# A two-layer hybrid decoder trunk on one core: no two-input GpSimd work, one gate moved inside a merge, and two matmul stages with the features outermost

## The chip, the cores and the metric

One core of a Trainium2 chip runs the whole program. Times are device microseconds (us) of one execution. PE is TensorE (PEld its weight loads), DVE VectorE, ACT ScalarE, POOL GpSimd, SP SyncE, which issues nearly all DMAs. Lower is better.

## The reference, cut to what matters

The input x is 256 tokens of 1024 features in float32. Each of two layers does:

```python
h = rmsnorm(x, mix_norm)
ret, fox, rwkv, gate = split(h @ w_in)               # 1024, 772, 1024, 3072 columns
y = retention(ret), forgetting_attention(fox), rwkv7(rwkv)   # 256 columns each
merged = sum(sigmoid(gate[b]) * (y[b] @ p[b]) for b in range(3))
x = x + merged @ w_out
h = rmsnorm(x, ffn_norm)
x = x + (silu(h @ w_gate) * (h @ w_up)) @ w_down      # 2816 columns in between
```

In the RWKV branch the columns are first mixed with those of the token before: `cols + (prev - cols) * mu`.

## The kernel before, in words

**Layout and precision.** Activations are kept with the features on the partitions: x is four tiles `x0_0` to `x0_3` of 128 x (2 x 256), two blocks of 128 features in each. A product is made from three fp32r matmuls on split operands (`mm3`, L286): a high part (`whi`, `xh`) rounded by an ACT copy, a low part (`wlo`, `xl`) left over by a DVE subtraction, and hi x hi + hi x lo + lo x hi into one accumulator. A block is one 128x128 piece of weights with its three matmuls of 256 columns; a pair (`gemm_pair`, L296) is two output blocks over all eight feature blocks, 16 blocks or 48 matmuls, into one accumulator tile. Another order is `gemm_halves` (L308): with `kcut` it runs the feature blocks below the cut for both outputs first, then the rest.

**Weights.** `weights` (L222) yields all weight tiles in the order of use. `_piece` (L256) starts the DMA of the next tile on SP's queue (three buffers `raw`, 1 MB for 16 blocks) and splits eight blocks: an ACT cast to `whi` (L273), a DVE subtraction to `wlo` (L274), in four buffers each. `refill` (L280) keeps three split pieces ahead of the matmuls.

**Order.** The kernel is written as a list of operations; a scheduler orders each engine's queue at build time, by priority (roughly the order of writing; `early` raises it) and by what it expects to be ready. Each queue then runs strictly in that order, with semaphores. The RWKV, FoX and retention branches are generators that `mixers` (L496) interleaves with the dense matmuls of `gemms` (L529) by written-out costs (`PACE`); `self.need` makes it finish a branch before the merge that uses it.

**The stages of a layer.** (a) The norm is folded in afterwards: `norm_start`, `norm_add` (L384) scale and split x, `norm_sum` adds squares, `rstd` (L409) sums over partitions with the `pn` matmuls and takes an inverse root on DVE, `replicate` (L426) spreads it with the `pss` matmul. (b) Four RWKV pairs (`mixers`, L500 to L507, and `rwkv_in`, L622): the first as `gemm_halves` with a cut at 7, each needing all of x; then `rwkv_in` scales by rstd and mixes with the previous token, where POOL makes `dd` (L644) and DVE the rest (L633). (c) FoX (`fox_in`, L963; `mqk`, `mv`), retention (`ret_in`) and twelve gate pairs, with the branches in between. In `rwkv` (L655) POOL makes `k2` (L730), copies of v (L735), `rs` (L740) and `nn` (L786); the bonus matmul `pb` (L748) waits for `rkk` (L745, DVE); `lora` is loaded at L668 and used by `pw` (L673). In `ret` (L1103) the four `rsw` DMAs shift `rqk`, `cs` is loaded, POOL multiplies by the cosine (L1116), DVE by the sine (L1117). (d) Gates in the order of the branches; behind the second branch's gates the merges of branches 0 and 1, behind the third's four gates the four merges of branch 2, 12 matmuls each (L564). A merge is `(gate + 1) * ps` on DVE (L567), an addition (L569) on POOL, for branch 2 from the second tile on on DVE, and for branch 2 a split into `hi` and `lo` (L572), whose `lo` of the first tile is on POOL. (e) w_out (`layer`, L482): four pairs over the merged tiles, the first with a cut at 4, the last as halves. (f) The FFN.

**The start.** A memset tile feeds 30 dummy matmuls (L169). SP issues `x0_0`, the parameters, half of the first weight tile, `x0_1`, the other half, `x0_2`, `x0_3` (L175 to L183), then the next tiles and the constants (`load_rest`).

Of the kernel before, what the change touches and what calls it, by code (L numbers as in the profile page):

```python
# [91 lines left out]
def pack_inputs(inp, depth=DEPTH):  # L92
# [40 lines left out]
    out["win"] = np.ascontiguousarray(np.stack(win))  # L133
# [17 lines left out]
class Kernel:  # L151
    def __init__(self, ctx, tc, d, depth=DEPTH, debug=None):
# [16 lines left out]
        for _ in range(30):  # L169
# [4 lines left out]
        self.xt = [self.xp.tile([P, 2, T], F32, tag="x", bufs=5, name=f"x0_{j}") for j in range(4)]  # L174
        nc.sync.dma_start(self.xt[0], d["xt"][:, 0:2, :])  # L175
        nc.sync.dma_start(par[0], d["par"][0, :, 0:P_RES])
        self.jobs, self.raws, self.ready, self.cur = list(self.weights()), [], [], []
        w0 = self.raw.tile([P, 2080], F32, tag="raw", name=self.nm("raw"))
        for j in range(4):
            if j:  # L180
                nc.sync.dma_start(self.xt[j], d["xt"][:, 2 * j:2 * j + 2, :])
            if j < 2:
                nc.sync.dma_start(w0[:, 1024 * j:1024 * (j + 1)], d["win"][0, 0, :, 1024 * j:1024 * (j + 1)])  # L183
        self.jobs[0:1] = [(w0, 4, P, 0), (w0, 4, P, 4), (w0, 8, P, 8)]
# [123 lines left out]
    def gemm_halves(self, xs, kcut=None, hook=None, tag="mm"):  # L308
# [14 lines left out]
        for lo, hi in ((0, kcut), (kcut, n)):  # L323
# [139 lines left out]
    def layer(self, l):  # L463
        tc, nc, d = self.tc, self.nc, self.d
        if l == 0:
            self.norm_start(0, "mixg")
            for j in range(4):
                self.norm_add(j, False)
                if j != 2:
                    self.piece()  # L470
        xs = self.xs
        with ExitStack() as st:
# [23 lines left out]
    def mixers(self, l, xs):  # L496
# [3 lines left out]
        ps = [self.gemm_halves(xs, 7, tag="rw")]  # L500
        if l == 0:
            self.load_rest()
        for _ in range(1):
            ps.append(self.run(self.gemm_pair(xs)))
        rn, dg = self.rstd()
        ps.append(self.run(self.gemm_pair(xs)))
        rstd = self.replicate(dg)  # L507
# [21 lines left out]
    def gemms(self, l, xs, rstd, rn):  # L529
# [11 lines left out]
        gates = {}  # L541
        for b in (0, 1, 2):
            for c in range(4):
                gen = self.gemm_pair(xs)
                while True:
                    try:
                        next(gen)
                    except StopIteration as e:
                        ps = e.value
                        break  # L550
                    yield PACE["gemms3"]
                g = gates[b, c] = self.big.tile([P, 2, T], F32, tag="gate", bufs=8, name=self.nm("gate"))
                nc.vector.tensor_tensor(out=g, in0=ps, in1=self.b2(rstd), op=ALU.mult)  # L553
                nc.scalar.activation(g, g, AF.Tanh, scale=0.5)
                yield PACE["gemms3"]
            if b == 0:
                continue
            for bb in ((0, 1) if b == 1 else (2,)):
                self.need = ("ret", "fox", "rwkv")[bb]
                yield PACE["gemms4"]  # L560
                self.need = None
                y = [(self.y[bb][0][:, k, :], self.y[bb][1][:, k, :]) for k in range(2)]
                for c in range(4):
                    ps = self.run(self.gemm_pair(y))  # L564
                    g, m = gates[bb, c], gates[0, c]
                    with self.early("hp_merge"):
                        nc.vector.scalar_tensor_tensor(out=g, in0=g, scalar=1.0, in1=ps, op0=ALU.add, op1=ALU.mult)  # L567
                        if bb:
                            (nc.vector if bb == 2 and c >= 1 else nc.gpsimd).tensor_tensor(out=m, in0=m, in1=g, op=ALU.add)  # L569
                    if bb == 2:  # L570
                        with self.early("hp_turn"):
                            hi, lo = self.split(self.t2, m, [P, 2, T], ("t2", "t2"), nc.gpsimd if c < 1 else nc.vector)  # L572
                        self.mx.extend((hi[:, i, :], lo[:, i, :]) for i in range(2))
                    elif c % 2:
                        yield PACE["gemms5"]

# [45 lines left out]
    def rwkv_in(self, l, xs, rstd, first):  # L622
        nc = self.nc
        rav = self.big.tile([P, 2 * NC, 3 * C], F32, tag="q6", bufs=1, name=self.nm("rav"))
        r = self.t512("r")
# [5 lines left out]
        def mix(j, pj, dd):  # L631
            for i in range(2):
# [564 lines left out]
```

## Time and profile before

| | us |
|---|---|
| median of three runs | 800.0 (799.88 to 800.56) |
| profiled execution, its own time | 800.76 |
| its span, first to last instruction | 799.0 |
| PE busy | 783.6 (98%) |
| DVE busy | 576.2 (72%) |
| ACT busy | 397.1 (50%) |
| POOL busy | 61.6 (8%) |

Matmul records overlap: each lasts longer than the distance to the next one's start, so a busy PE can still change its pace, and a hole between two records is shorter than the time that was lost. The other engines run one instruction after the other.

### The profile page before, as it was taken

The numbers are of one execution on the slowest core, as the hardware profiler recorded it, in microseconds if no ns is written. First come the engines' busy times: TensorE is split into PE (matmuls) and PEld (weight loads), VectorE is DVE, ScalarE is ACT, GpSimd is POOL, SyncE is SP. The second block draws the span as 40 slices with busy tenths as digits, with TensorE's granted clock in tenths as the row PEclk, the third lists the DMA queues.
The fourth block names the chain that finished last, engine by engine and source line by source line (L and its number), as shares of the span: only waits on it lengthen the run. The fifth ranks groups of instructions, "written<-read, shape, count | busy, mean of one in ns | idle before, by whom it ended". The sixth has DMA issues, their size and how long they took to land.

```text
span 799.0 us, 16543 instructions
## 1 busy us (share of the span) xinstructions
PE 783.6 (98%) x7018; PEld 762.5 (95%) x7018; DVE 576.2 (72%) x900; ACT 397.1 (50%) x543; POOL 61.6 (8%) x83
## 2 busy tenths in 40 slices
PE   8999899999999999999999999999999999999998
PEld 6999899999999999999998988999999999999997
DVE  5897979597867666656678798877878666666453
ACT  6367445535645444445444764554456545444331
POOL 3201210031000000000023030101110000000000
PEclk9999999999999999999999999999999999999999
DMA  8565524335454554556554553452445454555650
GB/s 308 208 226 167 170 80 169 140 114 205 161 208 167 203 205 172 191 184 211 200 188 175 197 172 106 162 174 106 142 176 190 180 201 174 206 202 164 211 190 27
DMA packets 27802, 140.42 MB, mean 176 GB/s; under 512 B 7600, under 2 KB 9168, under 8 KB 12496
## 3 DMA queue, kind: packets, MB, share of 16 engines
q1 hardware_dynamic: 27728, 139.36, 50.2%
q8 instruction: 55, 0.90, 0.5%
q14 instruction: 19, 0.16, 0.1%
HBM read 136.97 MB, written 1.33 MB: 173 GB/s over the span
## 4 chain that ended last, share of the span: by engine, by line
PE 88%; DVE 6%; DMA 2%; ACT 1%; issue 1%; POOL 1%; SPq 0%; POOLq 0%; DVEq 0%; ACTq 0%
PE mm L290 26%; PE mm L294 25%; PE mm L293 25%; DVE wlo L274 2%; PE mqk L439 1%; PE mqk L438 1%; PE mqk L437 1%; ACT whi L273 1%; DMA rsw<-rqk 1%; PE pgm L762 1%; DVE rkk L745 1%; DMA raw<-in_win 1%; DMA raw<-in_pp 1%; PE mv L437 1%; PE mv L439 1%
## 5 line engine op out<-in xcount | busy, mean ns | idle before, releaser
L273 ACT CAST whi<-raw 128x1024 fp32r<-128x1024 f32 (+1 forms) x257 | 264.7, 1033 | 321.7 <-PE mm L293 232.2
L274 DVE TENSOR_TENSOR wlo<-raw,whi 128x1024 fp32r<-128x1024 f32 (+1 forms) x257 | 313.3, 1221 | 143.0 <-ACT whi L273 142.3
L290 PE MATMUL mm<-xh,whi 128*128 128x256 f32 x1312 | 368.0, 280 | 0.5 <-ACT whi L273 0.5
L294 PE MATMUL mm<-xh,wlo 128*128 128x256 f32 x1248 | 346.3, 277 | 0.7 <-DVE wlo L274 0.7
L293 PE MATMUL mm<-xl,whi 128*128 128x256 f32 x1248 | 346.3, 278 | 0.0
L290 PEld LDWEIGHTS mm<-xh,whi 128*128 128x128 f32 x1312 | 246.6, 188 | 2.8 <-issue 0.9
L294 PEld LDWEIGHTS mm<-xh,wlo 128*128 128x128 f32 x1248 | 234.4, 188 | 1.1 <-DVE wlo L274 0.9
L293 PEld LDWEIGHTS mm<-xl,whi 128*128 128x128 f32 x1248 | 234.5, 188 | 0.8 <-issue 0.5
L290 PE MATMUL mm<-hi,whi 128*128 128x256 f32 x576 | 160.1, 279 | 0.0
L294 PE MATMUL mm<-hi,wlo 128*128 128x256 f32 x544 | 150.9, 277 | 0.0
L293 PE MATMUL mm<-lo,whi 128*128 128x256 f32 x544 | 150.8, 277 | 0.0
L290 PEld LDWEIGHTS mm<-hi,whi 128*128 128x128 f32 x576 | 108.2, 188 | 0.6 <-issue 0.3
L294 PEld LDWEIGHTS mm<-hi,wlo 128*128 128x128 f32 x544 | 102.1, 188 | 0.2
L293 PEld LDWEIGHTS mm<-lo,whi 128*128 128x128 f32 x544 | 102.1, 188 | 0.1
L569 POOL TENSOR_TENSOR gate<-gate,gate 128x512 f32<-128x512 f32 x10 | 13.3, 1336 | 142.3 <-DVE gate L567 142.3
L600 DVE TENSOR_TENSOR h<-t,mm 128x512 f32<-128x512 f32 x22 | 15.1, 687 | 11.5 <-PE mm L294 8.6
L567 DVE SCALAR_TENSOR_TENSOR gate<-gate,mm 128x512 f32<-128x512 f32 x24 | 16.1, 682 | 8.6 <-PE mm L294 8.5
L597 DVE TENSOR_TENSOR t<-mm,rstd 128x512 f32<-128x512 f32 (+1 forms) x24 | 15.2, 645 | 8.5 <-PE mm L294 8.5
L553 DVE TENSOR_TENSOR gate<-mm,rstd 128x512 f32<-128x512 f32 x24 | 16.5, 689 | 3.8 <-PE mm L294 3.5
L293 PE MATMUL mm<-xh,wlo 128*128 128x256 f32 x64 | 18.0, 281 | 0.7 <-DVE wlo L274 0.7
L439 PE MATMUL mv<-whi,xl 128*128 128x260 f32 (+1 forms) x64 | 18.6, 290 | 0.0
L437 PE MATMUL mv<-whi,xh 128*128 128x260 f32 (+1 forms) x64 | 18.6, 290 | 0.0
(259 smaller groups left out, 797.9 us busy)
## 6 DMA issues: line engine op xcount, KB each, us to landing
raw<-in_wg SPq DMA_DIRECT2D x44, 1024.0 KB, 4.7
raw<-in_wgate SPq DMA_DIRECT2D x24, 1024.0 KB, 4.8
raw<-in_wd SPq DMA_DIRECT2D x16, 1024.0 KB, 5.0
raw<-in_win SPq DMA_DIRECT2D x13, 1024.0 KB, 8.0
raw<-in_wo SPq DMA_DIRECT2D x8, 1024.0 KB, 4.8
raw<-in_pp SPq DMA_DIRECT2D x6, 1024.0 KB
raw<-in_wd SPq DMA_DIRECT2D x8, 768.0 KB, 4.3
raw<-in_wqk SPq DMA_DIRECT2D x4, 1024.0 KB, 5.0
```

Source lines behind the costliest of these rows:

```text
L273: nc.scalar.copy(hi[:, :m * width], r)
L274: nc.vector.tensor_tensor(out=lo[:, :m * width], in0=r, in1=hi[:, :m * width].bitcast(F32), op=ALU.subtract)
L290: nc.tensor.matmul(out, wh, xh, start=first, stop=False)
L293: nc.tensor.matmul(out, wh, xl, start=False, stop=False)
L294: nc.tensor.matmul(out, wl, xh, start=False, stop=last)
L437: nc.tensor.matmul(out, xh[:, s], wh, start=first, stop=False)
L439: nc.tensor.matmul(out, xl[:, s], wh, start=False, stop=last)
L553: nc.vector.tensor_tensor(out=g, in0=ps, in1=self.b2(rstd), op=ALU.mult)
L567: nc.vector.scalar_tensor_tensor(out=g, in0=g, scalar=1.0, in1=ps, op0=ALU.add, op1=ALU.mult)
L569: (nc.vector if bb == 2 and c >= 1 else nc.gpsimd).tensor_tensor(out=m, in0=m, in1=g, op=ALU.add)
L597: nc.vector.tensor_tensor(out=t[:, o, :], in0=p, in1=self.bs(rstd, o), op=ALU.mult)
L600: nc.vector.tensor_tensor(out=h, in0=t, in1=pu, op=ALU.mult)
```

## The change

1. The first three weight tiles of layer 0's four RWKV pairs (and the fourth) are repacked, and `first_pairs` runs the four pairs with the feature blocks outermost: two feature blocks for all eight outputs, then the next two. `norm_add` of x tile 1, 2, 3 and `load_rest` are written between them, `rstd` and `replicate` inside the last quarter. The first quarter of the first tile is issued from ACT's queue; 22 dummy matmuls instead of 30.
2. `gemm_quad` runs w_out's first two pairs in the same manner, in both layers.
3. The last gate (branch 2, tile 3) moves behind the first two merges of branch 2; the RWKV projection's weights are loaded in two halves.
4. POOL's two-input work goes to DVE, its copies of v to ACT, and the token mixing becomes an ACT scaling by 1 - mu and one DVE operation. POOL keeps memsets and small one-input work.
5. `lora` is loaded at the top of `rwkv_in`.

```diff
-        for _ in range(30):
+        for _ in range(22):
             nc.tensor.matmul(pz, zero[:, 0:P], zero, start=True, stop=True)
...
+        nc.scalar.dma_start(w[0][:, 0:512], d["win0"][0, :, 0:512])
         nc.sync.dma_start(self.xt[0], d["xt"][:, 0:2, :])
         nc.sync.dma_start(par[0], d["par"][0, :, 0:P_RES])
...
+        nc.sync.dma_start(w[0][:, 512:1024], d["win0"][0, :, 512:1024])
+        nc.sync.dma_start(w[0][:, 1024:2048], d["win0"][0, :, 1024:2048])
+        for j in range(1, 4):
+            nc.sync.dma_start(self.xt[j], d["xt"][:, 2 * j:2 * j + 2, :])
+            if j < 3:
+                nc.sync.dma_start(w[j][:, 0:2048], d["win0"][j])
+        self.jobs[0:3] = [(w[0], 4, P, 0), (w[0], 4, P, 4), (w[0], 8, P, 8), (w[1], 16, P, 0), (w[2], 16, P, 0)]
...
+    def first_pairs(self, xs):
+        ps = [self.ps.tile([P, 2, T], F32, tag=t, bufs=n, name=self.nm("mm")) for t, n in (("rw", 2), ("rw", 2), ("mm", 4), ("mm", 4))]
+        for kk in range(4):
+            if kk < 3:
+                self.norm_add(kk + 1, False)
+            if kk == 2:
+                self.load_rest()
+            for j in range(4):
+                if kk == 3 and j == 1:
+                    rn, dg = self.rstd()
+                if kk == 3 and j == 3:
+                    rstd = self.replicate(dg)
+                for m in range(2):
+                    for k in range(2 * kk, 2 * kk + 2):
+                        if not self.cur:
+                            self.refill()
+                        self.mm3(ps[j][:, m, :], self.block(), xs[k], k == m == 0, k == KT - 1 and m == 1)
+        return ps, rn, rstd
+
+    def gemm_quad(self, xs):
+        ps = [self.ps.tile([P, 2, T], F32, tag="mm", bufs=4, name=self.nm("mm")) for _ in range(2)]
+        for kk in range(KT // 2):
+            for j in range(2):
+                for m in range(2):
+                    for k in range(2 * kk, 2 * kk + 2):
...
+                        self.mm3(ps[j][:, m, :], self.block(), xs[k], k == m == 0, k == KT - 1 and m == 1)
...
                 if j == 0:
-                    ps = self.gemm_halves(mx, 4)
...
+                    both = self.gemm_quad(mx)
+                ps = both[j] if j < 2 else self.run(self.gemm_pair(mx)) if j == 2 else self.gemm_halves(mx)
...
+        def merge(bb, c):
...
+                nc.vector.scalar_tensor_tensor(out=g, in0=g, scalar=1.0, in1=ps, op0=ALU.add, op1=ALU.mult)
+                if bb:
+                    nc.vector.tensor_tensor(out=m, in0=m, in1=g, op=ALU.add)
+            if bb == 2:
+                with self.early("hp_turn"):
+                    hi, lo = self.split(self.t2, m, [P, 2, T], ("t2", "t2"))
...
         for b in (0, 1, 2):
             for c in range(4):
+                if b == 2 and c == 3:
+                    self.need = "rwkv"
+                    yield PACE["gemms4"]
+                    self.need = None
+                    for m in (0, 1):
+                        merge(2, m)
+                for _ in gate(b, c):
                     yield PACE["gemms3"]
...
+        for c in (2, 3):
+            merge(2, c)
...
+        lora = self.t512("lora")
+        nc.sync.dma_start(lora.rearrange("p a t -> p (a t)"), self.d["par"][l, :, P_RES:])
...
+        nc.gpsimd.tensor_scalar(out=om, in0=self.prm(l, "mu", 0, 8), scalar1=-1.0, scalar2=1.0, op0=ALU.mult, op1=ALU.add)
...
-            nc.gpsimd.tensor_tensor(out=dd, in0=pj[:, :, 0:T], in1=pj[:, :, 1:], op=ALU.subtract)
...
+            for i in range(2):
+                n = 2 * j + i
+                nc.scalar.activation(dst[j][:, i, :], pj[:, i, 1:], AF.Identity, scale=om[:, n:n + 1])
+                nc.vector.scalar_tensor_tensor(out=dst[j][:, i, :], in0=pj[:, i, 0:T], scalar=self.prm(l, "mu", n),
+                                               in1=dst[j][:, i, :], op0=ALU.mult, op1=ALU.add)
...
-        nc.gpsimd.tensor_tensor(out=k2, in0=k2, in1=k, op=ALU.mult)
+        nc.vector.tensor_tensor(out=k2, in0=k2, in1=k, op=ALU.mult)
...
-            nc.gpsimd.tensor_copy(rav[hs[h], :, (2 - h) * C:(3 - h) * C], ch(v)[hs[h]])
+            nc.scalar.copy(rav[hs[h], :, (2 - h) * C:(3 - h) * C], ch(v)[hs[h]])
...
-        nc.gpsimd.tensor_tensor(out=rs[:, :, 1:, :], in0=r4[:, :, 1:, 0:C], in1=pend, op=ALU.mult)
+        nc.vector.tensor_tensor(out=rs[:, :, 1:, :], in0=r4[:, :, 1:, 0:C], in1=pend, op=ALU.mult)
...
-            nc.gpsimd.tensor_tensor(out=nn[hs[h]], in0=gg[hs[h], h::2, 2 * C:],
+            nc.vector.tensor_tensor(out=nn[hs[h]], in0=gg[hs[h], h::2, 2 * C:],
...
-        nc.gpsimd.tensor_tensor(out=qk, in0=qk, in1=b4(cs[:, 0, :]), op=ALU.mult)
+        nc.vector.tensor_tensor(out=qk, in0=qk, in1=b4(cs[:, 0, :]), op=ALU.mult)
```

## Rows read from the trace of the kernel before

**Rows 1.** The page, parts 1 and 2: busy time, share and instructions of each engine; the granted clock of PE in 40 slices, in tenths (9 is 90% or more).

```profile
PE 783.6 (98%) x7018; PEld 762.5 (95%) x7018; DVE 576.2 (72%) x900; ACT 397.1 (50%) x543; POOL 61.6 (8%) x83
...
PEclk9999999999999999999999999999999999999999
```

**Rows 2.** The page, part 4: the chain of work that ended last, by engine.

```profile
PE 88%; DVE 6%; DMA 2%; ACT 1%; issue 1%; POOL 1%; SPq 0%; POOLq 0%; DVEq 0%; ACTq 0%
```

**Rows 3.** The waits of PE: total us, how many, the longest.

```profile
PE mm L294 <- POOL lo L377: 3.1, 2, 1.6
PE pb L748 <- DVE rkk L745: 2.9, 2, 1.5
PE px L1068 <- DVE lg L1064: 1.5, 2, 0.7
```

**Rows 4.** Stretches of the span (us): length, busy time and number of instructions on PE, PEld, DVE, ACT and POOL, the granted clock, the DMA engines' share, GB/s.

```profile
343.00:350.00 7.00, 7.00 (x61) 7.00 (x61) 4.10 (x5) 2.84 (x4) 0.00 (x0) 1.00 0.51 186
260.00:340.00 80.00, 80.00 (x709) 80.00 (x708) 50.69 (x52) 38.50 (x45) 0.00 (x0) 1.00 0.54 192
200.00:206.00 6.00, 6.00 (x53) 6.00 (x52) 4.15 (x7) 1.88 (x3) 0.11 (x1) 1.00 0.38 134
```

**Rows 5.** The timeline of PE: start, duration, instruction, idle time before it and what ended it.

```profile
1.05 6.15 PE L170 MATMUL pz<-zero 128*128 128x256 bf16 x30 [1.05 <-DVE zero L167]
7.67 0.39 PE L290 MATMUL mm<-xh,whi 128*128 128x256 f32 x1 [0.46 <-ACT whi L273]
...
34.16 0.39 PE L437 MATMUL mqk<-whi,xh 128*128 128x512 f32 x1
```

**Rows 6.** The timeline of all engines at the start: SP's issue of the first x tile, ACT's first work on it, ACT's first split of weights.

```profile
0.74 0.39 SPq L175 DMA_DIRECT2D x<-in_xt  x1
...
4.03 0.63 ACT L403 ACTIVATE acc<-x 128x512 f32<-128x512 f32 x1 [2.02 <-DMA x<-in_xt]
...
7.00 0.62 ACT L273 CAST whi<-raw 128x512 fp32r<-128x512 f32 x1 [1.94 <-DMA raw<-in_win]
```

**Rows 7.** Stretches of the start, columns as in rows 4; the last is GB/s.

```profile
3.00:4.00 1.00, 1.00 (x6) 0.70 (x5) 0.00 (x0) 0.00 (x0) 0.94 (x3) 1.00 1.00 230
...
8.00:10.00 2.00, 1.38 (x9) 1.12 (x9) 2.00 (x5) 2.00 (x5) 0.00 (x0) 1.00 1.08 371
```

**Rows 8.** Groups of instructions by line: busy us, mean ns of one, idle us before them. Here ACT's scaling of 128x256.

```profile
L392 ACT ACTIVATE xh<-x,par 128x256 fp32r<-128x256 f32 x32 | 15.0, 502 | 3.2 <-DVE x L611 1.7 <-DVE x L491 1.3
```

**Rows 9.** The dummy matmuls alone in a stretch: busy time and number on PE and PEld, granted clock, DMA share, GB/s. One of the 26 is cut by the window's edge.

```profile
1.20:6.50 5.30, 5.30 (x26) 3.76 (x25) 1.00 0.76 197
```

**Rows 10.** The timelines of PE and of DVE around the norm: the `pn` matmuls, and the two `dg` that `replicate` needs.

```profile
21.98 0.50 PE L419 MATMUL pn<-con,tot 128*128 128x1 f32 x4
...
26.91 0.48 DVE L423 TENSOR_SCALAR dg<-con,y 128x128 f32<-128x128 f32 x2
```

**Rows 11.** Groups of instructions by line, columns as in rows 8: POOL's merges and cosine product, DVE's subtraction of the same shape as a merge.

```profile
L569 POOL TENSOR_TENSOR gate<-gate,gate 128x512 f32<-128x512 f32 x10 | 13.3, 1336 | 142.3 <-DVE gate L567 142.3
L1116 POOL TENSOR_TENSOR rqk<-rqk,cs 128x1024 f32<-128x1024 f32 x2 | 5.0, 2494 | 5.9 <-DMA cs<-in_const 5.9
L377 DVE TENSOR_TENSOR lo<-h,hi 128x512 fp32r<-128x512 f32 x22 | 15.1, 685 | 0.0
```

**Rows 12.** The instructions of line 745: duration in ns, least, median and most, and the first and last start.

```profile
L745 DVE SCALAR_TENSOR_TENSOR rkk<-r,par,k x4: 471/1536/2608, 84.3 to 478.6; 128x256 f32<-128x256 f32 x4
```

**Rows 13.** The timelines of DVE and of POOL from 77 us on (layer 0), columns as in rows 5.

```profile
77.77 0.69 DVE L723 SCALAR_TENSOR_TENSOR ka<-ta,kkr 128x512 f32<-128x512 f32 x1
...
78.58 0.88 DVE L1064 TENSOR_SCALAR lg<-lg,rc 128x128 f32<-128x128 f32 x4
79.38 2.38 DVE L725 SCALAR_TENSOR_TENSOR bk<-ka,pinv 64x512 f32<-64x512 f32 x2
81.77 1.39 DVE L732 TENSOR_TENSOR bk<-k,pinv 64x512 f32<-64x512 f32 x2
...
84.31 3.00 DVE L745 SCALAR_TENSOR_TENSOR rkk<-r,par,k 128x256 f32<-128x256 f32 x2
...
90.61 1.13 DVE L1064 TENSOR_SCALAR lg<-lg,rc 128x256 f32<-128x256 f32 x4
...
96.03 1.22 DVE L1117 TENSOR_TENSOR rsw<-rsw,cs 128x1024 f32<-128x1024 f32 x1
...
79.30 1.91 POOL L730 TENSOR_TENSOR k<-k,k 128x512 f32<-128x512 f32 x1 [7.47 <-ACT k L729]
84.18 2.45 POOL L1116 TENSOR_TENSOR rqk<-rqk,cs 128x1024 f32<-128x1024 f32 x1 [2.98 <-DMA cs<-in_const]
```

**Rows 14.** Stretches of layer 0's mixers, columns as in rows 4; the third pair of numbers is DVE.

```profile
30.00:65.00 35.00, 35.00 (x245) 31.73 (x243) 30.78 (x55) 20.80 (x31) 6.05 (x8) 1.00 0.50 183
65.00:95.00 30.00, 27.77 (x232) 26.37 (x230) 26.68 (x49) 18.48 (x39) 7.10 (x4) 1.00 0.56 179
```

**Rows 15.** The timelines of DVE, PE and POOL around layer 0's last merges: the low half of RWKV's output, the first merge matmul, the POOL subtraction, and the w_out matmul that waits.

```profile
186.39 0.69 DVE L377 TENSOR_TENSOR lo<-yn,hi 128x512 fp32r<-128x512 f32 x1
...
192.19 0.28 PE L290 MATMUL mm<-hi,whi 128*128 128x256 f32 x1
...
197.43 2.09 POOL L377 TENSOR_TENSOR lo<-gate,hi 128x512 fp32r<-128x512 f32 x1 [0.73 <-ACT hi L376]
...
199.57 0.39 PE L294 MATMUL mm<-lo,whi 128*128 128x256 f32 x1 [1.55 <-POOL lo L377]
```

More of the change, by code (lines that the diff above doesn't have):

```diff
@@ L466, in layer @@
             self.norm_start(0, "mixg")
[L467 to L470, printed above, removed]
+            self.norm_add(0, False)
+            self.piece()
         xs = self.xs
@@ L499, in mixers @@
         self.need = None
-        ps = [self.gemm_halves(xs, 7, tag="rw")]
         if l == 0:
-            self.load_rest()
-        for _ in range(1):
+            ps, rn, rstd = self.first_pairs(xs)
+        else:
+            ps = [self.gemm_halves(xs, 7, tag="rw"), self.run(self.gemm_pair(xs))]
+            rn, dg = self.rstd()
             ps.append(self.run(self.gemm_pair(xs)))
-        rn, dg = self.rstd()
-        ps.append(self.run(self.gemm_pair(xs)))
-        rstd = self.replicate(dg)
+            rstd = self.replicate(dg)
         rw = self.rwkv_in(l, xs, rstd, ps)
@@ L541, in gemms, with gate @@
         gates = {}
+        def gate(b, c):
+            ps = yield from self.gemm_pair(xs)
+            g = gates[b, c] = self.big.tile([P, 2, T], F32, tag="gate", bufs=8, name=self.nm("gate"))
+            nc.vector.tensor_tensor(out=g, in0=ps, in1=self.b2(rstd), op=ALU.mult)
+            nc.scalar.activation(g, g, AF.Tanh, scale=0.5)
+            yield
+        def merge(bb, c):
+            y = [(self.y[bb][0][:, k, :], self.y[bb][1][:, k, :]) for k in range(2)]
+            ps = self.run(self.gemm_pair(y))
+            g, m = gates[bb, c], gates[0, c]
+            with self.early("hp_merge"):
+                nc.vector.scalar_tensor_tensor(out=g, in0=g, scalar=1.0, in1=ps, op0=ALU.add, op1=ALU.mult)
[4 more added lines that the diff above has]
+                    hi, lo = self.split(self.t2, m, [P, 2, T], ("t2", "t2"))
+                self.mx.extend((hi[:, i, :], lo[:, i, :]) for i in range(2))
@@ L554, in gemms @@
[L554 to L559, printed above, removed]
+                if b == 2 and c == 3:
+                    self.need = "rwkv"
[4 more added lines that the diff above has]
+                for _ in gate(b, c):
+                    yield PACE["gemms3"]
@@ L560, in gemms @@
+            for bb in range(2) if b == 1 else ():
+                self.need = ("ret", "fox")[bb]
                 yield PACE["gemms4"]
                 self.need = None
-                y = [(self.y[bb][0][:, k, :], self.y[bb][1][:, k, :]) for k in range(2)]
                 for c in range(4):
[L564 to L574, printed above, removed]
+                    merge(bb, c)
+                    if c % 2:
@@ L629, in rwkv_in @@
         dst = [r, k, v, wg]
[L631 to L636 removed]
+        om = self.sm.tile([P, 8], F32, name="om")
+        nc.gpsimd.tensor_scalar(out=om, in0=self.prm(l, "mu", 0, 8), scalar1=-1.0, scalar2=1.0, op0=ALU.mult, op1=ALU.add)
         for j in range(4):
```

57 lines of the change are left out of this document (20 added, 37 removed).

## The prediction

> **What bounds the kernel now.** I read the page first: PE is busy for 783.6 of 799.0 us and the granted clock stands at its full 2.4 GHz in every slice [rows 1]; the chain of work that ended last is 88% PE and 6% DVE [rows 2]. So the kernel is a stream of matmuls with few holes, and a change is worth what it closes of the holes or does to the pace. The profiled execution took 800.76 us for its span of 799.0; the median of the three runs is 800.0. I make the sum against the span and move the median by the same amount.
>
> The view of waits names the holes behind the start [rows 3]: 3.1 us for POOL's subtraction in the last merge, 2.9 for `rkk` ahead of the RWKV bonus matmul, 1.5 for `lg` in FoX, each twice, once a layer. These are idle times between records; a 256-column matmul is recorded as 0.28 us long though the next starts about 0.118 after it, so each wait costs some 0.15 us more: 3.4, 3.2 and 1.8, together 8.4 us.
>
> The pace has two values that the page hides. In 260 to 340 us 709 matmuls are counted in 80 us, in 343 to 350 us 61 in 7 us [rows 4]; less the two or three that each window cuts, that is 0.113 and 0.119 us for one. What sets it I can't read from the trace, so I carry it as an unknown.
>
> The third hole is the start. Real matmuls begin at 7.67 us, and the four RWKV pairs end where `mqk` begins, at 34.16 [rows 5]: 4 x 48 = 192 matmuls, at 0.1165 some 22.4 us, with 0.6 for the six small `pn` and `pss` matmuls 23.0. The stretch lasts 26.5, so 3.5 us of it are waits. PE's first work, 30 dummy matmuls, runs from 1.05 to 7.20.
>
> **The start, part by part.** Before, the first weights are half a tile (0.5 MB), third in SP's queue behind `x` and `par`; ACT splits them at 7.00, after 1.94 us of waiting for that DMA, though `x`, issued at 0.74, was there at 4.03 [rows 6]. After, the first transfer is a quarter tile (0.26 MB) from ACT's own queue, beside that of `x`. `x` took until 4.03; 0.26 MB more at 230 KB/us [rows 7] is 1.1 us if the two follow each other and nothing if they overlap: weights at 4.1 to 5.1. ACT then needs 0.62 for `whi` [rows 6] and 0.50 for `xh` [rows 8]: first matmul at 5.2 to 6.2. The 22 dummies, at (5.3 us / 25) = 0.213 each [rows 9], end at 5.74. I take 5.9, which is 1.8 us earlier. (0.213 for 256 columns is the 1.2 GHz level, whatever the clock column says there; a matmul or two at 5.9 may still run at it, 0.1 us each.)
>
> Of the 3.5 us of waits those for `x` should go: a pair taken by itself needs all of `x` within 24 matmuls, features outermost need one `x` tile and one tile of weights per 48 matmuls (5.6 us), 1.3 MB, and the queues carry 370 KB/us by then [rows 7]. Those for the first splits stay, as DVE still makes `xl` and `wlo` in turn. I take half: 1.7 us. Against it stands the norm: from `pn` at 21.98 to the end of the second `dg` at 27.39 takes 5.4 us on DVE [rows 10], covered now by a whole pair. After, `replicate` is written 24 matmuls (2.8 us) behind `rstd`. If PE keeps that place it waits 2.6; the scheduler, which draws each engine's order up at build time by what it expects to be ready, may put the pair's last 12 matmuls or FoX in front, and then nothing. I take 0.5. The start: 1.8 + 1.7 - 0.5 = 3.0 us; ends 5.5 (first matmul at 5.2, no waits) and -1 (nothing comes earlier, and part of that wait). The `lora` transfer, 0.26 MB, hides behind the mixers' transfers; its worst is 0.7 us of crowding at the start (0.26 MB at 370 KB/us).
>
> **POOL's work on DVE and ACT.** By the diff DVE takes over 10 merges and 2 splits (128x512), 2 `k2` (128x512), 4 `nn` (64x512), 2 `rqk` (128x1024), 2 `rs` (128x384). POOL took 1.34 for a merge and 2.49 for an `rqk`, DVE does 128x512 in 0.685 [rows 11], so DVE gains 18 x 0.69 + 2 x 1.37 + 2 x 0.51 = 16.1 us. But an instruction of POOL stops one of DVE: `rkk`, 471 ns at least, lasted 2608 at most [rows 12], the long one beside POOL's 2.45 us `rqk` from 84.18; the two `bk` at 79.38 took 2.38, not 2 x 0.69 = 1.37, beside POOL's `k2` [rows 13].
>
> From 77 to 91 us DVE is the path: `rkk` ends at 84.31 + 3.00 = 87.31 [rows 13]. After, the `bk` pair is 1.0 shorter and the `rkk` pair 3.00 - 2 x 0.47 = 2.06, while `k2` adds 0.69 and `rs` perhaps 0.5 ahead of them: 1.9 to 2.4 us earlier. That is more than the 1.6 that PE waits at the bonus matmul; the rest goes off the 0.9 at `lg`, which follows `rkk` on DVE. I take 2.1 per layer, 4.2 us; ends: 2.5 per layer (both waits), and -1 per layer, as the new order on DVE can also push `rkk` back. ACT's new work, 16 scalings of 0.50 [rows 8] and four copies, about 10 us, lies where PE has three split pieces (24 blocks, 8 us) in hand; without that cover it would cost up to 5 us a layer. DVE is 88 and 89% busy at 30 to 65 and 65 to 95 us [rows 14], which is why it counts that the stops go.
>
> **The merge.** PE waits until 199.57 for the POOL subtraction that began at 197.43 [rows 15]. After, merges 0 and 1 are followed by the last gate's pair (48 matmuls, 5.4 us), and merges 2 and 3 by 16 blocks (48 matmuls) that need tiles 0 and 1 alone, while two merges hold DVE for 2 x 3 x 0.69 = 4.1 us. Both are covered, so the 3.4 us go; next in line to be late is a split of weights, which shares DVE with the merges. But merge 0 now starts one pair earlier, at 192.19 - 5.44 = 186.75, and the low half of RWKV's output is done at 186.39 + 0.69 = 187.08 [rows 15]: 0.3 us of waiting per layer. Net 2.8 us; ends 3.4 and 0. `pp` in two halves is one more SP issue per layer and costs nothing, as a tile's load runs a tile (5 us of PE) ahead. In the 384 matmuls that change their order (2 x 96 and 192) the pace can be either value: 0.005 x 384, up to 2 us; I put 0 and take 1 each way into the range.
>
> **Sum.** 3.0 + 4.2 + 2.8 = 10.0 us: span 789.0, median **790.0**.
>
> **Rivals.** (1) DVE's stretch does not improve, since its new order puts other work ahead of `rkk`: 794.2. For it: 88% busy; against: the measured stops. (2) The start stays as it was, held by transfers or by the norm: 793.0, with (1) 797.2. For it: 230 KB/us early on; against: `x` alone was there 3 us before the weights. (3) Slower: the cosine product at the head of DVE's queue. It needs `cs` and the four `rsw` transfers; POOL idled 2.98 us for them until 84.18 [rows 13]. Queued behind `ka` (77.77) it would hold DVE until 84.18 + 1.37 = 85.55, and then follow `lg` 0.80, `bk` 1.37, `k2` 0.69, the 2.54 from 81.77 to 84.31 and `rkk` 0.94: `rkk` ends at 91.9, 4.6 later than now, and PE stands at the bonus matmul with the splits queued behind it too. 800 - 3.0 - 2.8 + 2 x 4.6 = 803.4; it turns the sum from 2.9 us of lateness per layer on. Against it: its sibling at 96.03, which needs the same transfers, was queued well behind their landing [rows 13]. (4) The clock: outermost features change the accumulator every 6 matmuls. If PE fell to the 1.2 GHz level there, 384 matmuls would take 0.213 instead of 0.118 us: 36 us more, 826. Against it: w_out's first pair already goes to and fro between two accumulators at 200 to 206 us, with 53 matmuls counted at a granted clock of 1.00 [rows 4]. The Trainium skill (TensorE: Matmul & The Clock Gate, "A second HAM failure mode: psum-queue depth-cycling") tells of a kernel whose clock swung as it cycled through accumulators; by that rule (4) could happen, and the row shows none of it. (5) The scheduler's new order loses elsewhere in the mixers what the waits give: 800.
>
> **Chances.** Forecast 0.62; (1) 0.13; (2) 0.10; both 0.04; (3) 0.05; (4) 0.01; (5) 0.05. The range takes in (1), (2) and the unknown pace upwards, and half of what the good ends give (5.5 + 5.0 + 3.4 = 13.9 against 10.0) with the pace downwards: 786.5 to 795.5. A measurement of this kernel can tell about 0.2%, 1.6 us, from no change: faster 0.89 (forecast, 1, 2, both), same 0.05 (5), slower 0.06 (3, 4).
>
> **What would show it.** Right: the first real matmul near 5.9 and `mqk` near 31; no PE wait for `rkk` or for POOL; `rkk` at 0.47 throughout; the w_out matmuls following the merges without a hole. Wrong: PE idle ahead of `pss`; DVE idle ahead of the cosine product for `cs`; new PE waits for `whi` or `wlo` in the mixers; matmuls of 0.213 us, or a lower granted clock, after the start; the slow pace over longer stretches than now.

## The result, and the profile after

The changed kernel takes 795.57 us (median of 4 runs, 794.65 to 796.88) beside 800.24 for the kernel before (4 runs): ratio 0.9946, 95% interval 0.9933 to 0.9958. The profiled execution took 795.98 us, its span 794.0. It is faster, as forecast, but by 4.7 us and not by 10.

The page of the changed kernel, parts 1, 2 and 4, answers to [rows 1, 2]:

```profile
PE 785.9 (99%) x7010; PEld 761.8 (96%) x7010; DVE 569.4 (72%) x919; ACT 403.6 (51%) x563; POOL 15.0 (2%) x51
...
PEclk9999999999999999999999999999999999999999
...
PE 94%; DVE 2%; DMA 2%; ACT 1%; issue 0%; SPq 0%; DVEq 0%; ACTq 0%
```

POOL is nearly idle, DVE is no busier than before, the clock holds its 2.4 GHz level, and DVE's share of the chain falls from 6 to 2%. PE is busy for 2.3 us more than before with eight dummies fewer: the span shrank by less than the waits did, and something was added to PE's own time. The waits of PE (total us, how many, the longest), against [rows 3]:

```profile
PE mm L304 <- ACT whi L287: 1.3, 1, 1.3
PE pz L176 <- DVE zero L173: 1.1, 1, 1.1
PE par L935 <- ACT wa L927: 0.4, 2, 0.2
PE pn L887 <- DVE dn L882: 0.3, 2, 0.2
PE mm L304 <- ACT xh L440: 0.3, 1, 0.3
PE px L1113 <- DVE lg L1109: 0.2, 1, 0.2
```

The waits for POOL and for `rkk` are gone and that for `lg` nearly; `par` waits anew, and `pn`, which waited once for 0.2 us before, waits twice. `rkk` takes the same time in all four places, where [rows 12] spread from 471 to 2608 ns (least, median, most; first and last start):

```profile
L790 DVE SCALAR_TENSOR_TENSOR rkk<-r,par,k x4: 479/479/479, 82.0 to 473.0; 128x256 f32<-128x256 f32 x4
```

**Where the time went, by stage.** I take the first record of `mv`, `pvr` (the retention's norm), `pv` (RWKV's norm) and the FFN's `pss` in each layer of each profile, and subtract the kernel before. The last column runs to the start of the last matmul; the span of the changed kernel shrank by 0.2 us more behind it. The other stages (layer 0's FFN, layer 1's RWKV pairs, the last FFN) differ by 0.00 in every run.

```
us against before   start>mv  mv>pvr L0, L1  pvr>pv L0, L1  pv>pss L0, L1   to the end
forecast              -3.0     -2.1   -2.1     0      0      -1.4   -1.4      -10.0
changed kernel        -1.98    -1.95  -1.46   +2.09  +1.68   -1.50  -1.69      -4.80
e1  GpSimd part       +0.54    -1.64  -1.45   +2.17  +1.68   +1.23  +2.83      +5.36
e2  start             -2.34    +5.00  -1.22   +0.85  -0.41   -0.01  -0.24      +1.63
e3  gate              -0.27    +0.14  +0.06   +0.05  +0.35   -1.02  -0.80      -1.48
e4  inversion first   -1.61    -1.83  -1.60   +1.89  +2.03   -1.69  -1.69      -4.51
e5  cosine            +0.24    -2.08  -2.11   +1.77  +1.28   -0.27  -0.25      -1.43
e6  cosine back       -2.12    -0.39  -0.08   +0.57  -0.15   -1.71  -1.69      -5.56
e7  lora late         -1.08    -1.69  -1.57   +2.48  +1.59   -1.50  -1.48      -3.25
e8  ACT queue         -1.57    -1.44  -1.60   +2.09  +1.71   -1.71  -1.67      -4.19
e9  paced             -2.19    -1.68  -1.63   -1.31  -2.08   +0.51  +0.54      -7.85
e10 inversion and py  -2.73    -1.75  -1.75   +0.83  +1.13   -1.69  -1.67      -7.63
e11 gate undone       -1.92    -1.82  -1.57   +2.18  +1.72   +3.14  +3.17      +4.90
e12 w_out order       +0.58    -0.03  -1.32   -0.17  +0.51   -0.14  -0.13      -0.71
```

Three stages gained (the merges more than forecast, the other two less), and one that I had at nothing, `pvr` to `pv`, took back 3.8 us. Each row is one profile, and the columns vary by themselves. At the start the eight profiles with the changed kernel's start give -1.1 to -2.7, the five with the old one (the kernel before among them) -0.3 to +0.6. From `pvr` to `pv` the four that have the old order of small matmuls there (e2, e3, e6, e12) give -0.41 to +0.85. The -1.22 and -1.32 of e2 and e12 in layer 1 are timing: neither changes this stage, but there `rkk` began just ahead of POOL's product and was not stopped (e12):

```profile
476.06 0.88 DVE L779 SCALAR_TENSOR_TENSOR rkk<-r,par,k 128x256 f32<-128x256 f32 x2
476.61 2.57 POOL L1150 TENSOR_TENSOR rqk<-rqk,cs 128x1024 f32<-128x1024 f32 x1 [3.65 <-DMA cs<-in_const]
```

In the profile of the kernel before, the product came first there (475.82 against 476.03), and `rkk` took 2.61 us. So the wait for `rkk` is not paid in every execution.

**The stage that lost.** The timeline of PE in the changed kernel (start, duration, instruction, idle time) where `pyr` and `ptr` lie (`pyr` is the retention's output; `ptr`, `pm`, `pn`, `par`, `pS` and `py` are RWKV's small matmuls, in this order):

```profile
103.14 0.43 PE L1191 MATMUL pyr<-rsc,rv 128*64 128x128 f32 x2
...
104.28 0.38 PE L1193 MATMUL pyr<-rsc,rv 128*64 128x128 f32 x2
104.59 0.99 PE L842 MATMUL ptr<-con,rav 128*128 128x128 f32 x6
105.52 0.43 PE L1191 MATMUL pyr<-rsc,rv 128*64 128x128 f32 x2
105.78 0.38 PE L1192 MATMUL pyr<-rsc,rv 128*64 128x128 f32 x2
106.10 0.44 PE L842 MATMUL ptr<-con,rav 128*128 128x128 f32 x2
106.46 0.43 PE L1193 MATMUL pyr<-rsc,rv 128*64 128x128 f32 x2
106.83 0.39 PE L308 MATMUL mm<-xh,wlo 128*128 128x256 f32 x1
```

in the kernel before:

```profile
106.59 0.43 PE L1146 MATMUL pyr<-rsc,rv 128*64 128x128 f32 x2
...
108.60 1.09 PE L797 MATMUL ptr<-con,rav 128*128 128x128 f32 x8
109.45 0.36 PE L293 MATMUL mm<-xl,whi 128*128 128x256 f32 x1
```

and in the changed kernel around `par`:

```profile
159.91 0.36 PE L308 MATMUL mm<-hi,wlo 128*128 128x256 f32 x1
160.48 0.87 PE L935 MATMUL par<-gg,wa 64*64 64x128 f32 x12 [0.20 <-ACT wa L927]
161.28 0.39 PE L304 MATMUL mm<-hi,whi 128*128 128x256 f32 x1
161.50 0.28 PE L307 MATMUL mm<-lo,whi 128*128 128x256 f32 x1
161.71 0.87 PE L935 MATMUL par<-gg,wa 64*64 64x128 f32 x12
```

No engine stands still here for long. The scheduler has cut the small matmuls into pieces and put them elsewhere: `ptr` in two pieces inside `pyr`, `par` in two with two dense ones between them, and the first `pn` matmuls, which stood right behind `pm`, 78 dense ones later. Each change of kind costs: `par` starts 0.21 us after the dense matmul ahead of it (161.50 to 161.71), and the second dense one behind a small group 0.22 after the first (161.28 to 161.50), where dense ones lie 0.113 to 0.118 apart. From the first `pyr` to the next dense matmul it is 3.69 us and was 2.86 (both layers); the largest single piece behind `pvr` is `py`:

```profile
168.31 0.69 PE L972 MATMUL py<-uw,gg 128*64 128x64 f32 x16
168.93 0.27 PE L980 MATMUL py<-us,ar 64*64 64x64 f32 x1
...
169.42 0.69 PE L972 MATMUL py<-uw,gg 128*64 128x64 f32 x16
170.03 0.27 PE L980 MATMUL py<-us,ar 64*64 64x64 f32 x1
...
170.64 0.38 PE L304 MATMUL mm<-xh,whi 128*128 128x256 f32 x1
```

Nearly all of one accumulator, then the other: 2.33 us. The same 56 matmuls in the sixth run below, in the order of the kernel before:

```profile
168.84 1.15 PE L972 MATMUL py<-uw,gg 128*64 128x64 f32 x32
169.92 0.27 PE L980 MATMUL py<-us,ar 64*64 64x64 f32 x2
...
170.20 0.40 PE L980 MATMUL py<-S,ar 64*64 64x64 f32 x10
170.53 0.39 PE L304 MATMUL mm<-xh,whi 128*128 128x256 f32 x1
```

1.69 us: the 24 matmuls of L980 take 0.61 when the two halves of 64 rows alternate and 0.49 + 0.61 = 1.10 when they don't (by the starts of the records, 0.15 of the 0.49 is one more change of kind).

**Theories.** A: the new order of small matmuls takes back what the freed DVE gave. B: the order costs nothing; the loss lies in the start, the gate, w_out or DVE's time. The order is written when the kernel is built and can be read from it without a run; between `pb` and `pv`, of the parts, that for GpSimd alone changes it. In that part the cosine product's move brings the pieces at `ptr`, `pn` and `par` (e5 below); the halves of `py` come with the merges' additions (e4 beside e10).

### The profile page after: what moved, and what is told of

It reads as the page before. It is cut to its first block, busy times and chain, and to the rows that moved or that the text cites. A ratio compares the mean times of both kernels' runs of the same rounds, so it can differ in the third digit from the quotient of the medians.

```text
span 794.0 us, 16539 instructions
## 1 busy us (share of the span) xinstructions
PE 785.9 (99%) x7010; PEld 761.8 (96%) x7010; DVE 569.4 (72%) x919; ACT 403.6 (51%) x563; POOL 15.0 (2%) x51
## 4 chain that ended last, share of the span: by engine, by line
PE 94%; DVE 2%; DMA 2%; ACT 1%; issue 0%; SPq 0%; DVEq 0%; ACTq 0%
PE mm L304 27%; PE mm L307 27%; PE mm L308 27%; DVE wlo L288 1%; PE mqk L487 1%; PE mqk L486 1%; PE mqk L485 1%; DMA raw<-in_win 1%; ACT whi L287 1%; PE mv L485 1%; PE pgm L807 1%; PE mv L486 1%; PE mv L487 1%; DMA rsw<-rqk 1%; PE ptr L842 1%; PE psc L1183 0%
## 5 line engine op out<-in xcount | busy, mean ns | idle before, releaser
L288 DVE TENSOR_TENSOR wlo<-raw,whi 128x1024 fp32r<-128x1024 f32 (+1 forms) x257 | 308.7, 1203 | 152.0 <-ACT whi L287 151.4
L308 PE MATMUL mm<-xh,wlo 128*128 128x256 f32 x1264 | 351.0, 278 | 0.1
L307 PE MATMUL mm<-xl,whi 128*128 128x256 f32 x1264 | 350.6, 277 | 0.1
L307 PEld LDWEIGHTS mm<-xl,whi 128*128 128x128 f32 x1264 | 237.5, 188 | 1.4 <-issue 0.5
L307 PE MATMUL mm<-lo,whi 128*128 128x256 f32 x576 | 160.2, 278 | 0.2
L308 PE MATMUL mm<-hi,wlo 128*128 128x256 f32 x576 | 160.2, 278 | 0.0
L307 PEld LDWEIGHTS mm<-lo,whi 128*128 128x128 f32 x576 | 108.2, 188 | 1.0 <-DVE lo L425 0.6
L308 PEld LDWEIGHTS mm<-hi,wlo 128*128 128x128 f32 x576 | 108.1, 188 | 0.3
L486 PE MATMUL mv<-wlo,xh 128*128 128x260 f32 (+1 forms) x64 | 18.4, 287 | 0.0
L440 ACT ACTIVATE xh<-x,par 128x256 fp32r<-128x256 f32 x32 | 14.8, 501 | 2.5 <-DVE x L661 1.7
```

Of the source, the lines that this page charges most:

```text
L288: nc.vector.tensor_tensor(out=lo[:, :m * width], in0=r, in1=hi[:, :m * width].bitcast(F32), op=ALU.subtract)
L307: nc.tensor.matmul(out, wh, xl, start=False, stop=False)
L308: nc.tensor.matmul(out, wl, xh, start=False, stop=last)
L486: nc.tensor.matmul(out, xh[:, s], wl, start=False, stop=False)
```

## The experiments

Twelve kernels, five rounds each, in three sets that shared their runs of the kernel before (medians 800.66, 800.04, 800.21).

**e1, the GpSimd part alone**, in the kernel before (item 4 of the change):

```diff
-            nc.gpsimd.tensor_tensor(out=dd, in0=pj[:, :, 0:T], in1=pj[:, :, 1:], op=ALU.subtract)
+                nc.scalar.activation(dst[j][:, i, :], pj[:, i, 1:], AF.Identity, scale=om[:, n:n + 1])
...
-                            (nc.vector if bb == 2 and c >= 1 else nc.gpsimd).tensor_tensor(out=m, in0=m, in1=g, op=ALU.add)
+                            nc.vector.tensor_tensor(out=m, in0=m, in1=g, op=ALU.add)
...
-        nc.gpsimd.tensor_tensor(out=k2, in0=k2, in1=k, op=ALU.mult)
+        nc.vector.tensor_tensor(out=k2, in0=k2, in1=k, op=ALU.mult)
```

> The kernel before with part 4 alone (two-input GpSimd work to DVE, copies of v and the token mixing to ACT and DVE, merges' additions on DVE); start, w_out, gate and lora as before. Theory A (the stretch of DVE gains about 2 us a layer, but the build-time order of RWKV's small matmuls, which changes with this part alone, gives back 2.1 + 0.8 us in layer 0 and 1.7 + 0.8 in layer 1 between the retention's output and pv): no net gain from the mixers; the addition on DVE instead of POOL may give up to 1 us a merge: 798.0 to 801.0. PE's run of 24 pn matmuls right behind pm is gone and a run of 78 dense matmuls stands there. Rival B (the order costs nothing; the loss lies in the start, the gate or w_out): 800.2 - 4.2 to - 6: 794 to 796.

806.83 us, 1.0082 [1.0065, 1.0100]: outside both. The mixers come out as A has it (-1.64 + 2.17, -1.45 + 1.68), but the merges got worse. Its waits of PE, columns as above:

```profile
PE mm L296 <- DVE lo L413: 4.0, 2, 2.0
PE mm L292 <- DVE gate L591: 1.4, 2, 0.7
```

With POOL's additions and splits on DVE, and four merges in a row, DVE itself is late at w_out, later than POOL was.

**e2, the start alone**, in the kernel before (item 1):

```diff
-        for _ in range(30):
+        for _ in range(22):
...
+            ps, rn, rstd = self.first_pairs(xs)
```

> The kernel before with the start alone (first_pairs, packed first tiles, 22 dummies). Theory A: the start gives the 2.0 us by which mv and pw come earlier in the trace of the changed kernel, and nothing else moves, as the order behind it is that of before: 798.2. Rival (the start gave the 3.0 us predicted and some of it was lost again later, in the mixers): 797.2 or less here. Rival (the start gives nothing by itself): 800.2.

803.88, 1.0035 [1.0023, 1.0048]. The start gave its 2.3 us by `mv`, then 5.0 were lost, most of them in these waits of PE:

```profile
...
PE mm L299 <- DVE fn L1018: 2.5, 1, 2.5
...
PE pw L712 <- DMA lora<-in_par: 1.3, 1, 1.3
```

The earlier PE meets work of DVE and a load that are later: `fn` begins at 54.3 us (51.1 before), and `lora` is issued at 43.1 (38.8 before). What holds them up was not separated. "Nothing else moves" was wrong.

**e3, the gate alone**, in the kernel before (item 3; POOL keeps its first addition and split):

```diff
+                if b == 2 and c == 3:
+                    self.need = "rwkv"
...
+                    for m in (0, 1):
+                        merge(2, m)
```

> The kernel before with the gate moved behind the first two merges and the last projection's weights in halves; POOL keeps its addition and its split of the first tile. If the cover of one pair is what takes the wait away: PE's 3.1 us at POOL's subtraction goes although POOL still does it, 0.3 a layer comes back ahead of the first merge: 797.0 to 797.6. If the wait goes only because the work left POOL: 799 to 800.2. If the moved gate costs elsewhere: over 800.2.

798.68, 0.9980 [0.9971, 0.9989], between the first two times that it allowed: the wait for POOL is gone with POOL still at work, so cover takes it away; 0.9 a layer, less than the 1.4 expected, since the second merge's `lo` is late next (0.53 us between two starts at 201.45).

**e4, the inversion raised in priority** on top of the changed kernel:

```diff
         for i in range(1, Q):
             n = i + 1
+            with self.tc.high_priority(120):
...
```

> The changed kernel with one thing more: the inversion steps of RWKV (the loop of products and sums into ti, DVE, 30 small instructions a layer) are raised in the scheduler's priority by 120, so that they come ahead of the retention's last steps on DVE again; DVE and POOL do the same work as in the changed kernel. Theory A: the pn matmuls come right behind pm again, wa is early at par, groups of 24 dense matmuls stand between the small ones; of the 2.1 and 1.7 us lost there most comes back, the 0.8 us at ptr and pyr stays: 795.6 - 2.5 to - 3.8 = 791.8 to 793.1. Rival B (the order costs nothing): 795.6. Rival C (steps of the inversion ahead of the splits make PE wait for wlo): 796 or more.

796.25, 0.9954 [0.9939, 0.9969]: no gain, a miss for A as I had put it. The time is that of rival C, but not by its mechanism: PE has no wait for `wlo` here. The wait at `par` went, but `py` stayed h by h and was cut once more, and `pn` stayed in pieces; `pvr` to `pv` is +1.89 and +2.03. Part of the order was mended, and not the part that costs most.

**e5, the cosine product alone on DVE**, in the kernel before:

```diff
-        nc.gpsimd.tensor_tensor(out=qk, in0=qk, in1=b4(cs[:, 0, :]), op=ALU.mult)
+        nc.vector.tensor_tensor(out=qk, in0=qk, in1=b4(cs[:, 0, :]), op=ALU.mult)
```

> The kernel before with one instruction a layer moved: the retention's cosine product from GpSimd to DVE. The scheduler answers with the order of small matmuls of the changed kernel (ptr between pyr, 78 dense matmuls between pm and pn, pn and par in pieces). Theory A (that order costs 0.8 us a layer at ptr and pyr and 2.1 and 1.7 us between the retention's output and pv, and it comes from this one product): the wait for rkk goes, 1.6 to 2.2 us a layer, the order costs 2.9 and 2.5: 800.2 - 3.2 to - 4.4 + 5.4 = 801.2 to 802.4. Rival B (the order costs nothing): 795.8 to 797.

799.55, 0.9991 [0.9982, 1.0000]: 1.6 us below A's interval, 2.5 above B's. B is out, and A's pattern is there, at a lower price: -2.1 a layer up to `pvr`, +1.77 and +1.28 behind it. One instruction a layer does both. The halves of `py` are not its doing; here `py` takes 1.74 us:

```profile
170.66 1.20 PE L962 MATMUL py<-uw,gg 128*64 128x64 f32 x32
...
172.40 0.38 PE L292 MATMUL mm<-xh,whi 128*128 128x256 f32 x1
```

**e6, the cosine product back on POOL**, in the changed kernel, with the merges' first additions:

```diff
-        nc.vector.tensor_tensor(out=qk, in0=qk, in1=b4(cs[:, 0, :]), op=ALU.mult)
+        nc.gpsimd.tensor_tensor(out=qk, in0=qk, in1=b4(cs[:, 0, :]), op=ALU.mult)
...
-                    nc.vector.tensor_tensor(out=m, in0=m, in1=g, op=ALU.add)
+                    (nc.vector if bb == 2 and c >= 1 else nc.gpsimd).tensor_tensor(out=m, in0=m, in1=g, op=ALU.add)
```

> The changed kernel with the cosine product, and the merges' additions of branches 0 and 1 and of the first tile of branch 2 (with its split), back on GpSimd; k2, the copies, rs, nn and the mixing stay off it. The order of the small matmuls from pgm to pv is then that of the kernel before. Theory A: the order's 2.9 and 2.5 us come back; against them rkk may again stand beside GpSimd's product, 0 to 2.2 us a layer: 790.2 to 794.6; pyr and ptr as before (2.86 us from the first pyr to the next dense matmul, not 3.69), py 1.69 and not 2.32. Rival B (the order costs nothing): 795.6 to 800.

795.11, 0.9931 [0.9918, 0.9943], 0.5 us above A's interval and below B's. The stages decide: `pvr` to `pv` falls from +2.09, +1.68 to +0.57, -0.15, and `mv` to `pvr` from -1.95, -1.46 to -0.39, -0.08, since PE waits for `rkk` again, which stands beside the product on POOL (the wait; then the instructions of the two lines, as above):

```profile
PE pb L793 <- DVE rkk L790: 2.9, 2, 1.5
```

```profile
L790 DVE SCALAR_TENSOR_TENSOR rkk<-r,par,k x4: 477/1534/2654, 81.9 to 472.7; 128x256 f32<-128x256 f32 x4
```

```profile
L1161 POOL TENSOR_TENSOR rqk<-rqk,cs x2: 2370/2380/2391, 82.2 to 472.7; 128x1024 f32<-128x1024 f32 x2
```

The two stages together are +0.18 and -0.23 here, +0.14 and +0.22 in the changed kernel: what this edit moves costs about the same on either engine, once as a lock and once as an order. It moves the additions too, and with them the 0.63 us of `py`; of the product alone e5 says -0.31 and -0.83 for its move to DVE.

**e7, lora late**, in the changed kernel:

```diff
-        lora = self.t512("lora")
-        nc.sync.dma_start(lora.rearrange("p a t -> p (a t)"), self.d["par"][l, :, P_RES:])
...
+        lora = self.t512("lora")
+        nc.sync.dma_start(fl(lora), self.d["par"][l, :, P_RES:])
         w2a2, g2 = lora[:, 0, :], lora[:, 1, :]
```

> The changed kernel with lora loaded where the kernel before loads it, ahead of pw. In the run with the start alone pw waited for lora in layer 0, and the next dense matmul behind it for DVE: 4.3 us of idle PE. Theory A (the start needs the early load): the same here, 795.6 + 4 to 5.3 = 799.6 to 801. Rival (those waits belong to the mixing and to GpSimd's work, which this kernel no longer has): 795.6.

796.24, 0.9954 [0.9942, 0.9967]. The rival holds: nothing waits at `pw`. Loading `lora` early is worth nothing clear of noise here, and the waits of e2 are gone with the other parts. That GpSimd's part is the one that takes them away is likely, but not shown: no run has the start and that part alone.

**e8, the second quarter on ACT's queue too**, in the changed kernel:

```diff
-        nc.sync.dma_start(w[0][:, 512:1024], d["win0"][0, :, 512:1024])
+        nc.scalar.dma_start(w[0][:, 512:1024], d["win0"][0, :, 512:1024])
```

> The changed kernel with the second quarter of the first weight tile issued from ACT's queue too, right behind the first quarter, and not as SP's third transfer. Theory (the wait of 1.61 us at 7.28 us is for that quarter, which lands at 8.2 because it stands behind x and the parameters on SP's queue): the wait shrinks by up to 1.3 us: 794.3 to 795. Rival (the 16 engines are full, and x or the first quarter lands later by as much): 795.6 or more.

796.71, 0.9960 [0.9946, 0.9974]. The rival holds. The wait for that quarter went, but `par`, behind `x` on SP's queue, landed later, and ACT's scaling needs it (5.68 in the changed kernel):

```profile
5.47 0.62 ACT L287 CAST whi<-raw 128x512 fp32r<-128x512 f32 x1 [2.53 <-DMA raw<-in_win]
...
6.96 0.91 ACT L440 ACTIVATE xh<-x,par 128x256 fp32r<-128x256 f32 x2 [0.87 <-DMA par<-in_par]
```

**e9, the order restored by pacing**, in the changed kernel (the product stays on DVE, the merges' first additions as in e6):

```diff
-'rwkv5': 0.99, 'rwkv6': 10.9, 'rwkv9': 15.39, 'rwkv17': 6.78, 'rwkv22': 8.91, 'rwkv23': 25.79, 'ret0': 2.57, 'ret1': 2.4
+'rwkv5': 1.54, 'rwkv6': 7.38, 'rwkv9': 16.83, 'rwkv17': 5.55, 'rwkv22': 12.53, 'rwkv23': 24.79, 'ret0': 4.42, 'ret1': 1.70
```

> The changed kernel with eight numbers of the pacing table changed (rwkv5 1.54, rwkv6 7.38, rwkv9 16.83, rwkv17 5.55, rwkv22 12.53, rwkv23 24.79, ret0 4.42, ret1 1.7) and the merges' additions of branches 0 and 1 and of the first tile of branch 2 (with its split) on GpSimd as before; the cosine product stays on DVE. The numbers were chosen by the order alone that the scheduler writes: ptr and pyr each in one run, pn right behind pm, par and pn whole, py alternating between its two accumulators. Theory A (what the mixers gave back is that order): 0.8 us a layer at ptr and pyr and 2.1 and 1.7 us between pvr and pv come back, while rkk stays free of GpSimd: 795.6 - 5.4 = 790.2, up to 791.5 if some of the new places wait. Rival B (what they gave back is DVE's time for the product or the late DMAs of the inversion, whatever the order): 795 to 796.

793.00, 0.9916 [0.9902, 0.9929]: faster than both kernels, the interval clear of the changed kernel's. `pv` stands 22 dense matmuls earlier, so its last two columns are read together: -0.80 and -1.54, where the changed kernel has +0.59 and -0.01. That is 2.9 us of the 5.4 expected; the rest went into waits at the new places:

```profile
PE pvr L416 <- ACT ex L413: 1.7, 2, 0.8
PE py L972 <- DVE S L962: 1.1, 4, 0.4
...
PE pv L998 <- DVE ysq L991: 0.5, 2, 0.3
```

B is out again: DVE has the product here as in the changed kernel. The additions on POOL explain little of the gain by themselves: e5 has them there too, with the pieces, and lost 1.77 and 1.28 from `pvr` to `pv`.

**e10, e4 with `py` alternating**: e4's edit and e6's second one, which brings that order.

> The kernel of the fourth run (inversion raised by 120) with the merges' additions of branches 0 and 1 and of the first tile of branch 2 (with its split) on GpSimd as before. The order from px to pv is then that of the kernel before, pS in two fours and py alternating; ptr and pyr, and pn in pieces behind pm, stay as in the changed kernel. If py's order (h by h, 2.32 us for 56 matmuls and not 1.69) and the pieces of pS cost what the records say: 0.8 us a layer less than the fourth run between pvr and pv, 794.6. If they cost nothing: 796.2.

794.70, 0.9929 [0.9916, 0.9941]. `py` takes 1.69 us, where e4 has 2.76. `pvr` to `pv` fell from +1.89, +2.03 to +0.83, +1.13, 1.0 a layer where 0.8 was expected. Against e4's time it is 1.6, though its profile also has the best of the starts.

**e11, the gate undone**, in the changed kernel:

```diff
-                if b == 2 and c == 3:
...
-            for bb in range(2) if b == 1 else ():
+            for bb in ((), (0, 1), (2,))[b]:
```

> The changed kernel with the gate back in its place and the last projection's weights in one tile; w_out's order and DVE's additions stay. In the run with GpSimd's work alone PE lost 0.98 + 2.40 us at the first merges of branch 2, where the kernel before lost 1.83. Theory A (DVE's additions and splits of four merges in a row are late at w_out, and only the moved pair covers them): pv to the FFN's pss goes from -1.5 and -1.7 us to +1.2 and up to +2.8 against the kernel before: 795.6 + 2.7 + 2.7 to 4.5 = 801 to 802.8. Rival (the gate is worth the 0.9 us a layer that it gave alone): 797.4.

805.21, 1.0064 [1.0047, 1.0080]: theory A, and more than it said. The moved pair is worth 4.6 and 4.9 us a layer here, where DVE does all of the merges and w_out has its new order, and 0.9 alone in e3. Its waits of PE:

```profile
PE mm L304 <- DVE lo L422: 6.7, 2, 3.3
```

**e12, w_out's order alone**, in the kernel before (item 2):

```diff
-                    ps = self.gemm_halves(mx, 4)
+                    both = self.gemm_quad(mx)
```

> The kernel before with w_out's first two pairs in the new order alone. The first 24 matmuls then need the first merged tile alone, which GpSimd finishes last: the wait of 1.83 us stays: 800.2, at most 0.5 to either side from the pace. Rival (it moves the other tiles' splits away from the path): 798.5.

800.58, 1.0003 [0.9994, 1.0012]: nothing, as expected. In its profile the timing of `rkk` in layer 1 gained 1.32, and the start and layer 1's `pvr` to `pv` took most of it back.

## Why the prediction was right in sign and wrong in size

**The step that failed** is the part "POOL's work on DVE and ACT". It followed DVE from 77 to 91 us, found 2.1 us a layer, and took the order of PE behind it as given. The waits it named did go: 1.6 at `pb` and 0.66 at `px` (0.36 us between two starts, was 1.02) are 2.3 a layer. But moving the product and the merges' additions redrew PE's queue for the rest of the branch: +0.83 a layer at `pyr` and `ptr`, which leaves 1.4 of the gain (1.46 was measured in layer 1, 1.95 in layer 0; the 0.5 more lies in small amounts all over the stretch), then +2.09 and +1.68. In layer 0's 2.09, `py` is 0.63, by the additions; the waits at `par` and `pn` are about 0.6 (0.57 and 0.43 between starts where 0.20 is usual), and the rest, by subtraction, is put down to the pieces. The mechanism stood there as rival (5), with a chance of 0.05 and as one that eats everything; it should have been a term with a price.

**The start** was mis-sized: 1.98, not 3.0 (2.0 on the average of the eight profiles with this start, so not this one's luck). First matmul 6.23, not 5.9, and the second quarter of the first tile, which I had not priced at all, was split only at 8.22:

```profile
5.15 0.62 ACT L287 CAST whi<-raw 128x512 fp32r<-128x512 f32 x1 [2.70 <-DMA raw<-in_win]
...
5.68 0.90 ACT L440 ACTIVATE xh<-x,par 128x256 fp32r<-128x256 f32 x2
...
6.23 0.58 PE L304 MATMUL mm<-xh,whi 128*128 128x256 f32 x1 [0.31 <-ACT xh L440]
...
8.22 0.62 ACT L287 CAST whi<-raw 128x512 fp32r<-128x512 f32 x1 [1.64 <-DMA raw<-in_win]
...
8.89 0.39 PE L304 MATMUL mm<-xh,whi 128*128 128x256 f32 x1 [1.33 <-ACT whi L287]
```

PE had four matmuls and then waited 1.3 us. e8 shows that another queue only shifts the lateness. The norm cost little, as taken: `pss` went in behind the first five `mqk` matmuls, at 32.82, with no wait recorded.

**The merge** came out right: -1.50 and -1.69 for -1.4, with the new 0.27 us (0.39 between starts at 184.92) for the low half of RWKV's output. What I did not see is how much the moved gate covers once DVE does the additions: without it the same kernel is 4.6 and 4.9 slower there (e11).

**The pace**, put at 0 with 1 us each way: by the starts of records 1098 dense matmuls follow each other at 0.116 to 0.124 us, before 1392; 294 x 0.0045 = 1.3 us gained. It is inside the stages above, and what sets it stays open.

The sum of misses: 1.0 at the start, 0.15 + 0.64 up to `pvr`, 2.09 + 1.68 behind it, less 0.4 at the merges: 5.2 us, the distance from 10.0 to 4.8. Two slips of the working changed little: 5.3 / 25 is 0.212, not 0.213, and the low end of the range comes to 787.1 by its own terms, not 786.5. Rivals (3) and (4) did not happen: the product ran at 91.5, far behind `rkk` at 82.0, and the clock stayed at its 2.4 GHz level in both new orders.

Whether the first place of the pieces (78 dense matmuls ahead of `pn`) costs by itself was not separated from the rest.

## What to carry to other kernels

Where a scheduler draws up the queues at build time, an instruction moved to another engine also moves everything that was placed around it: compare the written order of the critical engine before and after, count the pieces, and price them like waits. Parts of a change are not additive: GpSimd's part, the start and the gate alone measured +6.6, +2.8 and -1.6 us, and together with the two small parts -4.3 by their ratio. A cover such as the moved gate is worth what stands behind it, so cost it in the kernel in which it will stand.

## What the runs showed of the hardware

The stop between POOL and DVE is about as long as POOL's instruction: `rkk`, 477 ns at least in e6, took 2654 at most there, beside products of 2370 to 2391, and 479 everywhere once POOL was idle. A `rkk` that began before the product was not stopped (e12, layer 1). The Trainium skill (SBUF — State Buffer, "Who interferes with whom") calls the port pair of the two an exclusive lock; by that rule the loser stands for the whole instruction, and the rows agree.

Matmuls on 64 rows follow each other faster when their neighbours lie on the other half: 24 of them took 0.61 us alternating and 1.10 us half by half, 0.15 of it for one more change of kind. The Trainium skill (TensorE: Matmul & The Clock Gate, "Part 3: Packing small matmuls — row/col tiling") says that the loading of weights overlaps running matmuls only where their row groups differ; by that rule the order within a group of equal matmuls decides, and the rows agree.

The start's transfers land unevenly: with the same program at the start, in eight profiles, ACT's split of the second quarter began at 7.0 to 8.4 us, and `mv` came 1.1 to 2.7 us earlier than before.
